# Activation sums of a down projection's seven-product pairs kept in device memory, with ten such pairs in each half in place of seven

## The chip, the core and the metric

The kernel runs on one core of a Trainium2 chip. The profile names the core's engines: PE (TensorE, matrix multiply, with its weight loads shown as PEld), DVE (VectorE, elementwise work), ACT (ScalarE, elementwise functions and copies), POOL (GpSimd; here masks and a DMA queue) and SP (SyncE; here only a DMA queue). Each engine takes its own instructions in order, and semaphores tie them together. Data moves between device memory and on-chip memory by DMA; products are accumulated in PSUM, on-chip memory of eight banks of 128 x 512 numbers as this kernel uses it.

The metric is device time in microseconds (us) of one execution, lower is better. A run of the kernel gives one time, and the time of a kernel is the median of its runs. One further execution is profiled, and all rows of the profile are from it.

## The reference

The kernel computes one layer of a hybrid encoder on 256 positions with 2048 features, in float32, and a last norm. The first part (gated mixing, neighbourhood attention, their merge) is not touched. What matters here is the second part:

```python
def conv_ffn(x, g_norm, w_up, conv_k, conv_b, w_down):
    h = rms_norm(x, g_norm)
    up = h @ w_up
    t = up.shape[1]
    pad = jnp.pad(up, ((0, 0), (1, 1), (0, 0)))
    up = (pad[:, :t] * conv_k[0] + pad[:, 1:t + 1] * conv_k[1]
          + pad[:, 2:t + 2] * conv_k[2] + conv_b)
    gate, val = jnp.split(up, 2, axis=-1)
    return x + (jax.nn.silu(gate) * val) @ w_down
```

`w_up` is 2048 x 11008, `w_down` 5504 x 2048. The down projection multiplies a 256 x 5504 matrix of activations by `w_down`.

## The kernel before

**Splitting.** Each float32 operand is split into a high part, rounded to the type that PE multiplies (`fp32r` in the profile), and a low part, the difference. A product is then three matmuls, high by high, low by high and high by low, all added in PSUM. That is `triple` (L289 to L293). For weights the split is made in `split_to` (L130): ACT copies the raw weights `wraw` into `whi`, DVE subtracts and writes `wlo` (L151 and L152). Four buffers of each (`SPLIT_AHEAD + 1`) hold split weights, five (`LOAD_AHEAD`) hold raw ones.

**Pieces.** All weights are loaded in one list of pieces, in the order in which they are used. A piece of the down projection is 128 rows of `w_down` by 1024 columns, kept as two blocks of 512 columns. `begin(i)` starts piece i: it issues loads up to piece i + 4 on SP's queue, the split of piece i + 3, and then the tasks that were set for i with `at(i, ...)`. After that PE's matmuls of piece i are recorded. This is what sets each engine's order: nothing is rescheduled.

**The down projection.** It is run by `wide` and `run_wide` in two halves of 1024 columns each (`g_dn`). A half has 43 pieces: 21 pairs and a single piece. Of the output, four blocks are accumulated: two blocks t of 128 positions by two blocks c of 512 columns, in four banks C. A plain piece is four triples, one for each block, 12 matmuls; a plain pair 24. A pair whose position is in `DOWN_QUADS` is computed with seven products instead of eight, in the manner of Strassen's method as Winograd arranged it: sums of the two pieces' weight blocks and sums of the two activation blocks are multiplied, and four more banks P collect four of the products over all such pairs of the half. Such a pair is 3 triples in its first piece and 4 in its second, 21 matmuls.

Before, seven pairs of each half are done so, at positions 4, 6, 9, 11, 14, 16, 18 and 3, 5, 8, 10, 13, 15, 17. For a pair that begins with piece i there is this work:

- `act_sums` at i - 5 on DVE: high and low of the activations are added again (L298), and four sums and differences of 128 x 128 blocks are made (L300 to L303);
- `act_sums_split` at i - 4: these are split, by ACT (L309) and DVE (L310);
- `weight_sums` at i - 3: four sums and differences of 512-column blocks, on DVE (L316 to L319);
- `weight_sums_split` at i - 2: two splits of 1024 columns, on ACT (L326) and DVE (L327);
- of the pair's own first piece only one of the two blocks is split (`units`).

All results go into eight rooms of `hpool` (`h_room`), one for each name, which held the input of the up projection before. After the last such pair, `ev_sums` takes the four products P from their banks and adds them into the output `x2` in two parts (L909 to L914, L917 to L919). At the end of the first half `ev_down` adds the four banks C, squares the result for the last norm and multiplies it by that norm's weights (`columns`, L1022), which are loaded through POOL's queue (`load_fin`, two buffers). The last four pieces of the second half are walked block by block (`tail`), so that each block can be finished while PE works on the next.

**The up projection** comes before it: 22 groups of eight pieces; `ev_up` takes a group's banks and makes the convolution, the gate (`gate`) and the split activations `ff["a"]` for two blocks of 128 features, as tasks of the next group's pieces.

Of the kernel before, what the change touches and what calls it, by code (L numbers as in the profile page):

```python
# [8 lines left out]
F32 = mybir.dt.float32  # L9
# [48 lines left out]
Y_GAP = 224  # L58
DOWN_QUADS = ((4, 6, 9, 11, 14, 16, 18), (3, 5, 8, 10, 13, 15, 17))


@with_exitstack
def trunk_kernel(ctx, tc, x, norm_mix, w_in, ln_g, ln_b, w_s, b_s, rpb, w_branch, w_out,
# [202 lines left out]

    def wide(src, row0, order, c0, acts, quads, room, done, sums=None, odd=None):
# [21 lines left out]
    def triple(p, x, h, l, st, sp):  # L289
# [3 lines left out]
        nc.tensor.matmul(p, xh, l, start=False, stop=sp)  # L293

    def act_sums(a, box, room):
        w = room("f", F32)
        f = w[:, 0].rearrange("p (k t) -> p k t", k=2)
        nc.vector.tensor_add(f, a[:, :, 0, :].bitcast(F32), a[:, :, 1, :].bitcast(F32))  # L298
        s1, s2, s3, s4 = (w[:, 1, n * 128:(n + 1) * 128] for n in range(4))
        nc.vector.tensor_add(s1, f[:, 0, 128:], f[:, 1, 128:])  # L300
        nc.vector.tensor_sub(s3, f[:, 0, :128], f[:, 0, 128:])
        nc.vector.tensor_sub(s2, s1, f[:, 0, :128])
        nc.vector.tensor_sub(s4, f[:, 1, :128], s2)  # L303
        box["w"] = w

    def act_sums_split(box, room, name):
        w = box.pop("w")
        o = room(name, F32R)
        nc.scalar.activation(o[:, 0], w[:, 1], AF.Copy)  # L309
        nc.vector.tensor_sub(o[:, 1], w[:, 1], o[:, 0].bitcast(F32))  # L310
        box["s"] = [(o[:, 0, n * 128:(n + 1) * 128], o[:, 1, n * 128:(n + 1) * 128]) for n in range(4)]

    def weight_sums(i, box, room):
        r0, r1 = whole.pop(i), whole.pop(i + 1)
        t13, t24 = room("t13", F32), room("t24", F32)
        nc.vector.tensor_sub(t13[:, 0], r0[:, 1], r0[:, 0])  # L316
        nc.vector.tensor_sub(t24[:, 0], r1[:, 1], t13[:, 0])
        nc.vector.tensor_sub(t13[:, 1], r1[:, 1], r0[:, 1])
        nc.vector.tensor_sub(t24[:, 1], r1[:, 0], t24[:, 0])  # L319
        box["w"] = (t13, t24)  # L320

    def weight_sums_split(box, room):
        u = []
        for name, t in zip(("13", "24"), box.pop("w")):
            h, l = room("h" + name, F32R), room("l" + name, F32R)
            nc.scalar.activation(h, t, AF.Copy)  # L326
            nc.vector.tensor_sub(l, t, h.bitcast(F32))  # L327
            u.append((h, l))
        box["t"] = {1: [x[:, 0] for x in u[0]], 3: [x[:, 1] for x in u[0]],
                    2: [x[:, 0] for x in u[1]], 4: [x[:, 1] for x in u[1]]}  # L330

    def run_wide(g, tail=0):
# [12 lines left out]
        for i in range(n0, n1 - tail):  # L345
# [22 lines left out]
            S, W = boxes[q]["acts"]["s"], boxes[q]["t"]  # L368
            triple(P[1], S[0], *W[1], st, sp)
            triple(P[3], S[2], *W[3], st, sp)  # L370
            triple(P[2], S[1], *W[2], st, sp)
            triple(C[1][0], x_of(k1, 1), *W[4], False, False)
# [152 lines left out]
    def post_sums(P, x, spare):  # L525
        p1, p5, p6, p7 = P
        (x11, x12), (x21, x22) = x
        nc.scalar.activation(x11, p1, AF.Copy)
        nc.vector.tensor_add(spare, p6, x11)
        nc.vector.tensor_add(x12, p5, spare)  # L530
        nc.vector.tensor_add(x21, p7, spare)
        nc.vector.tensor_add(x22, p5, x21)

    def add_sums(ps, x):
        for t in range(NT):
            for c in range(2):
                nc.vector.tensor_add(x[t][c], ps[t][c], x[t][c])

# [360 lines left out]
    def ev_sums(j, room):  # L899
        def done(P, i):  # L900
            x2 = rs["x2"]
            p1, p5, p6, p7 = P
            x11, x12, x21, x22 = (x2[:, t, c * 512:(c + 1) * 512] for t in range(2) for c in (j, j + 1))
            m = {}

            def first_half():
                ab, cd = room("t13", F32), room("t24", F32)
                m["v"], m["u3"], m["w"] = cd[:, 0], cd[:, 1], ab[:, 0]
                nc.scalar.activation(ab[:, 0], p1, AF.Copy)  # L909
                nc.vector.tensor_add(x11, p1, x11)  # L910
                nc.vector.tensor_add(ab[:, 1], p6, ab[:, 0])
                nc.vector.tensor_add(m["v"], p5, ab[:, 1])
                nc.vector.tensor_add(m["u3"], p7, ab[:, 1])
                nc.vector.tensor_add(m["w"], p5, m["u3"])  # L914

            def second_half():
                nc.vector.tensor_add(x12, x12, m["v"])  # L917
                nc.vector.tensor_add(x21, x21, m["u3"])
                nc.vector.tensor_add(x22, x22, m["w"])  # L919

            at(i + 1, first_half)
            at(i + 2, second_half)
        return done
# [49 lines left out]
    def ev_up(f0, nb):  # L973
        def done(ps, i):
            n = nb
            a = []
            for p in ps:
                t = tmp.tile([128, T], F32, name="tb", bufs=3)
# [45 lines left out]
    def ev_down(ps, i):  # L1024
# [111 lines left out]
    h_room = {n: f"h{i}" for i, n in enumerate(("t13", "t24", "h13", "h24", "l13", "l24", "f", "s"))}  # L1136
# [113 lines left out]
    ff["ap"] = [fa.tile([128, min(2, NF - k), 2, T], F32R, name=f"a{k // 2}") for k in range(0, NF, 2)]  # L1250
    ff["a"] = [ff["ap"][k // 2][:, k % 2] for k in range(NF)]
    fc = {}

# [4 lines left out]
    for g in g_up:  # L1258
        run_group(g)
    def open_fin():  # L1260
        fc["st"].close()
# [47 lines left out]
```

## Time and profile before

The kernel before took 1316.88 us, median of 3 runs (1316.34 to 1316.91). Of the profiled execution the page gives the span from the first to the last instruction.

| what | us |
|---|---|
| time, median of 3 runs | 1316.88 |
| span of the profiled execution | 1314.9 |
| PE busy | 1303.3 (99%) |
| DVE busy | 1066.2 (81%) |
| ACT busy | 764.8 (58%) |
| POOL busy | 88.3 (7%) |

Rows of a timeline or a group read: start in us or the line, how long, the engine, the line of the code, the operation, what is written and read by the program's names, the shape, and how many alike. Square brackets give how long the engine sat idle ahead of the row and what ended that. A row of the busy time by stretch has the stretch, its length, then for each engine the busy time and the number of instructions, the granted clock of PE (1.00 is full), the share of time in which the DMA engines were busy, and what they moved in GB/s. A line of the DMA table has the number of issues, the size of one and the median time to landing. A row's duration and the distance to the next row's start are two things, since instructions of one engine overlap a little.

### The profile page before, as it was taken

To read this page: it belongs to the slowest core of one execution; us is meant where nothing else is said; L and a number is where in the kernel's file an instruction comes from. 1 tells how busy PE (TensorE), PEld (TensorE's weight loads), DVE (VectorE), ACT (ScalarE), POOL (GpSimd) and SP (SyncE) were. 2 spreads that over 40 slices of the span, in tenths; PEclk is the share of its full clock that TensorE was granted. 3 is DMA by queue.
4 is the path that set the end of the run, shared out by engine and by line. 5 is a ranking of instruction groups with operands and counts; after the bars stand their busy time and mean duration, and the time that the engine had idled before them with its cause. 6 is when DMAs were issued, how large, how long until landed. Compare 5 with 4: busy or idle time off the path is not lost.

```text
span 1314.9 us, 19329 instructions
## 1 busy us (share of the span) xinstructions
PE 1303.3 (99%) x6776; PEld 1112.0 (85%) x6776; DVE 1066.2 (81%) x1625; ACT 764.8 (58%) x1139; POOL 88.3 (7%) x176
## 2 busy tenths in 40 slices
PE   9999999999999999999999999999999999999997
PEld 7888888888888888888888888888888888888885
DVE  7996778667789966986777778787878789999997
ACT  5766476666645644556555555555656556555653
POOL 0004505323000000000000000000000000000000
PEclk9999999999999999999999999999999999999999
DMA  8768656556556657665565665656565656666663
GB/s 305 260 209 235 201 174 201 181 163 194 179 172 209 210 190 241 204 210 163 175 202 182 192 193 182 195 184 193 180 205 177 198 154 226 220 194 206 210 202 119
DMA packets 170577, 259.37 MB, mean 197 GB/s; under 512 B 12664, under 2 KB 124144, under 8 KB 170480
## 3 DMA queue, kind: packets, MB, share of 16 engines
q1 hardware_dynamic: 166448, 250.31, 59.4%
q0 software_dynamic: 3712, 7.30, 2.4%
q8 instruction: 53, 0.87, 0.3%
q10 hardware_dynamic: 320, 0.53, 0.1%
q14 instruction: 44, 0.36, 0.1%
HBM read 253.90 MB, written 2.10 MB: 195 GB/s over the span
## 4 chain that ended last, share of the span: by engine, by line
PE 97%; DVE 1%; ACT 0%; issue 0%; DMA 0%; ACTq 0%; DVEq 0%
PE bank L205 31%; PE bank L209 16%; PE bank L293 12%; PE bank L291 12%; PE bank L292 12%; PE bank L233 5%; PE bank L235 4%; PE bank L234 4%; PE bank L761 1%; DVE wlo L152 0%; PE bank L811 0%; PE bank L503 0%; PE bank L627 0%; PE bank L801 0%; PE bank L892 0%
## 5 line engine op out<-in xcount | busy, mean ns | idle before, releaser
L152 DVE TENSOR_TENSOR wlo<-wraw,whi 128x1024 fp32r<-128x1024 f32 (+1 forms) x472 | 550.3, 1178 | 188.7 <-ACT whi L151 92.0
L151 ACT ACTIVATE whi<-wraw 128x1024 fp32r<-128x1024 f32 (+1 forms) x472 | 472.0, 1015 | 204.7 <-PE bank L292 75.2
L205 PE MATMUL bank<-h,whi 128*128 128x512 f32 x1760 | 426.0, 392 | 0.0
L205 PEld LDWEIGHTS bank<-h,whi 128*128 128x128 f32 x1760 | 321.9, 188 | 62.0 <-DVE ya L631 0.3
L209 PEld LDWEIGHTS bank<-h,wlo 128*128 128x128 f32 x1760 | 225.9, 191 | 8.8
L209 PE MATMUL bank<-h,wlo 128*128 128x256 f32 x1760 | 228.6, 283 | 0.0
L989 ACT ACTIVATE tc<-ta,ck 128x256 f32<-128x256 f32 x86 | 47.1, 594 | 117.1 <-DVE ta L987 117.1
L293 PE MATMUL bank<-wlo,a 128*128 128x512 f32 x260 | 101.5, 390 | 0.2 <-DVE wlo L152 0.2
L292 PE MATMUL bank<-whi,a 128*128 128x512 f32 x260 | 101.2, 389 | 0.0
L291 PE MATMUL bank<-whi,a 128*128 128x512 f32 x260 | 101.2, 389 | 0.0
L291 PE MATMUL bank<-whi,h 128*128 128x512 f32 x204 | 80.3, 393 | 0.0
L292 PE MATMUL bank<-whi,h 128*128 128x512 f32 x204 | 79.5, 390 | 0.0
L293 PE MATMUL bank<-wlo,h 128*128 128x512 f32 x204 | 79.5, 390 | 0.0
L293 PEld LDWEIGHTS bank<-wlo,a 128*128 128x128 f32 x260 | 48.8, 188 | 11.2 <-DVE wlo L152 1.3
L292 PEld LDWEIGHTS bank<-whi,a 128*128 128x128 f32 x260 | 48.8, 188 | 10.3
L291 PEld LDWEIGHTS bank<-whi,a 128*128 128x128 f32 x260 | 48.8, 188 | 10.1
L992 DVE SCALAR_TENSOR_TENSOR tc<-ta,ck,tc 128x255 f32<-128x255 f32 x86 | 41.4, 481 | 14.5 <-ACT tc L989 14.5
L979 ACT ACTIVATE tb<-bank 128x256 f32<-128x256 f32 x86 | 28.3, 385 | 42.2 <-PE bank L205 42.2
L233 PE MATMUL bank<-whi,y 128*128 128x512 f32 x128 | 50.5, 394 | 0.0
L233 PE MATMUL bank<-whi,h 128*128 128x512 f32 x128 | 50.4, 394 | 0.0
L235 PE MATMUL bank<-wlo,h 128*128 128x512 f32 x128 | 49.9, 390 | 0.0
L235 PE MATMUL bank<-wlo,y 128*128 128x512 f32 x128 | 49.9, 390 | 0.0
(299 smaller groups left out, 1744.1 us busy)
## 6 DMA issues: line engine op xcount, KB each, us to landing
wraw<-in_w_up_dram SPq DMA_DIRECT2D x336, 256.0 KB, 3.2
wraw<-in_w_in_dram SPq DMA_DIRECT2D x111, 512.0 KB, 4.5
wraw<-in_w_down_dram SPq DMA_DIRECT2D x86, 512.0 KB, 4.6
wraw<-in_w_in_dram SPq DMA_DIRECT2D x66, 256.0 KB, 3.2
wraw<-in_w_branch_dram SPq DMA_DIRECT2D x32, 512.0 KB, 4.5
wraw<-in_w_out_dram SPq DMA_DIRECT2D x32, 512.0 KB, 3.6
xs<-in_x_dram SPq DMA_DIRECT2D x8, 256.0 KB, 7.6
vw<-y POOLq DMA_DIRECT2D x16, 128.0 KB, 6.9
```

The costliest lines, as they stand in the source:

```text
L151: nc.scalar.activation(h[:, k, :m], w[:, k, :m], AF.Copy)
L152: nc.vector.tensor_sub(l[:, k, :m], w[:, k, :m], h[:, k, :m].bitcast(F32))
L205: nc.tensor.matmul(p, h[:, k - k0, b * 128:(b + 1) * 128], acts(k), start=k == 0, stop=k == nk - 1)
L209: nc.tensor.matmul(p[:, :T], l[:, k - k0, b * 128:(b + 1) * 128], acts(k)[:, 0, :], start=False, stop=False)
L233: nc.tensor.matmul(p, xh, h[:, kk, :m], start=st, stop=False)
L234: nc.tensor.matmul(p, xl, h[:, kk, :m], start=False, stop=False)
L235: nc.tensor.matmul(p, xh, l[:, kk, :m], start=False, stop=sp)
L291: nc.tensor.matmul(p, xh, h, start=st, stop=False)
L292: nc.tensor.matmul(p, xl, h, start=False, stop=False)
L293: nc.tensor.matmul(p, xh, l, start=False, stop=sp)
L989: nc.scalar.activation(v, u, AF.Identity, scale=ck[:, 1, ch:ch + 1], bias=ck[:, 3, ch:ch + 1])
L992: nc.vector.scalar_tensor_tensor(v[:, 1:], u[:, :T - 1], ck[:, 0, ch:ch + 1], v[:, 1:], op0=OP.mult, op1=OP.add)
```

## The change

Four things change, and they belong together.

1. The activation sums are made once, in the up projection. When the second block of a pair has been gated, `sums` (two pieces later) makes the four sums of 128 x 128 blocks from the gated activations before they are split, `sums_split` (one piece after that) splits them and stores them to device memory through POOL's queue, for the ten pairs of `DOWN_PAIRS`. The down projection no longer calls `act_sums`; `stored`, set for piece i - 4, loads 512 KB of split sums back, through POOL's queue, into one of two rooms in turn. Each stored pair is used in both halves.
2. Each half now has ten pairs with seven products, at positions 3, 5, 7, 9, 10, 12, 14, 16, 17, 19 and 2, 4, 6, 8, 9, 11, 13, 14, 16, 18. `down_order` arranges the pieces of a half so that the ten stored pairs come to these positions.
3. The split weight sums have two sets of rooms, used in turn (`both_rooms`); the second is a pool opened at the start of the down projection.
4. The signs of the sums are chosen anew (adds for subtractions among the weight sums, and the reverse where products are put together), with as many operations as before. The last norm's weights are loaded three pieces later, and the memory that is set aside for the descriptors of POOL's DMAs is set to 2048 bytes of each partition, where it was left at its default.

```diff
-DOWN_QUADS = ((4, 6, 9, 11, 14, 16, 18), (3, 5, 8, 10, 13, 15, 17))
+DOWN_PAIRS = (3, 5, 7, 9, 10, 12, 14, 16, 17, 19)
+DOWN_QUADS = (DOWN_PAIRS, (2, 4, 6, 8, 9, 11, 13, 14, 16, 18))
...
-            own = odd if odd and n % 2 else room
+            own = odd if odd and n % 2 else split_room or room
...
-            if sums is None:
+            if stored:
                 b["acts"] = {}
-                sum_acts_at(i - 5, i - 4, b["acts"], lambda k=order[2 * q]: ff["ap"][k // 2], room, "s")
+                at(i - 4, lambda b=b, k=order[2 * q]: stored(k // 2, b["acts"]))
...
+    def act_blocks(w, a11, a21, a12, a22):
+        s3, n1, p2, s4 = (w[:, n * 128:(n + 1) * 128] for n in range(4))
+        nc.vector.tensor_sub(s3, a11, a21)
+        nc.vector.tensor_sub(n1, a22, a21)
+        nc.vector.tensor_add(p2, n1, a11)
+        nc.vector.tensor_sub(s4, a12, p2)
...
     def weight_sums(i, box, room):
         r0, r1 = whole.pop(i), whole.pop(i + 1)
         t13, t24 = room("t13", F32), room("t24", F32)
-        nc.vector.tensor_sub(t13[:, 0], r0[:, 1], r0[:, 0])
-        nc.vector.tensor_sub(t24[:, 0], r1[:, 1], t13[:, 0])
-        nc.vector.tensor_sub(t13[:, 1], r1[:, 1], r0[:, 1])
-        nc.vector.tensor_sub(t24[:, 1], r1[:, 0], t24[:, 0])
+        nc.vector.tensor_add(t13[:, 0], r0[:, 0], r0[:, 1])
+        nc.vector.tensor_add(t24[:, 1], t13[:, 0], r1[:, 1])
+        nc.vector.tensor_add(t13[:, 1], r0[:, 1], r1[:, 1])
+        nc.vector.tensor_add(t24[:, 0], r1[:, 0], t24[:, 1])
...
+                own[b] = g
+                if b and f0 // 2 in ff["kept"]:
+                    at(cur[0] + 2, sums)
+                    at(cur[0] + 3, sums_split)
+
+            def sums():
+                own["w"] = ff["more"].tile([128, 512], F32, name="sw")
+                act_blocks(own["w"], *(own[k][:, t * 128:(t + 1) * 128] for k in range(2) for t in range(2)))
+
+            def sums_split():
+                o = ff["more"].tile([128, 2, 512], F32R, name="so")
+                split_plain(own["w"], o)
+                nc.gpsimd.dma_start(ff["kept"][f0 // 2], o.bitcast(F32))
...
-            fin["load"]()
+            at(cur[0] + 3, fin["load"])
...
+    def both_rooms(name, dt):
+        n = ff[name] = ff.get(name, -1) + 1
+        return (ff["twice"] if n % 2 else hpool).tile([128, 2, 512], dt, name=h_room[name])
+
+    def stored(pair, box):
+        n = ff["turn"] = ff.get("turn", -1) + 1
+        o = down_room(f"s{n % 2}", F32R)
+        nc.gpsimd.dma_start(o.bitcast(F32), ff["kept"][pair])
+        box["s"] = sums_of(o)
+
+    def down_order(g):
+        free = [p for p in range(NF // 2) if p not in DOWN_PAIRS]
+        kept = list(DOWN_PAIRS)
+        pairs = [(kept if q in DOWN_QUADS[g] else free).pop(0) for q in range(NF // 2)]
+        return tuple(2 * p + kk for p in pairs for kk in range(2)) + (NF - 1,)
+
-    g_dn = [wide(w_d, 0, range(NF), g * 1024, lambda k: ff["a"][k], DOWN_QUADS[g], down_room,
-                 (ev_sums(2 * g, down_room), ev_down if g == 0 else finish)) for g in range(2)]
+    g_dn = [wide(w_d, 0, down_order(g), g * 1024, lambda k: ff["a"][k], DOWN_QUADS[g], down_room,
+                 (ev_sums(2 * g, down_room), ev_down if g == 0 else finish), stored=stored, split_room=both_rooms) for g in range(2)]
+    dram = keep("dram", space=bass.MemoryType.DRAM)
+    ff["kept"] = {p: dram.tile([128, 2, 512], F32, name=f"sums{p}") for p in DOWN_PAIRS}
...
-    nc = _bacc.Bacc("TRN2", target_bir_lowering=False, num_devices=1)
+    nc = _bacc.Bacc("TRN2", target_bir_lowering=False, num_devices=1, dynamic_dma_scratch_size=2048)
```

More of the change, by code (lines that the diff above doesn't have):

```diff
@@ L262, in run_group, with wide @@
             done(ps, b)
-    def wide(src, row0, order, c0, acts, quads, room, done, sums=None, odd=None):
+    def wide(src, row0, order, c0, acts, quads, room, done, sums=None, odd=None, stored=None, split_room=None):
         n0 = plan_wide(src, row0, order, c0)
@@ L298, in act_sums @@
         nc.vector.tensor_add(f, a[:, :, 0, :].bitcast(F32), a[:, :, 1, :].bitcast(F32))
[L299 to L303, printed above, removed]
+        act_blocks(w[:, 1], *(f[:, k, t * 128:(t + 1) * 128] for k in range(2) for t in range(2)))
         box["w"] = w
@@ L310, in act_sums_split, with sums_of @@
         nc.vector.tensor_sub(o[:, 1], w[:, 1], o[:, 0].bitcast(F32))
-        box["s"] = [(o[:, 0, n * 128:(n + 1) * 128], o[:, 1, n * 128:(n + 1) * 128]) for n in range(4)]
+        box["s"] = sums_of(o)
+    def sums_of(o):
+        return [(o[:, 0, n * 128:(n + 1) * 128], o[:, 1, n * 128:(n + 1) * 128]) for n in range(4)]
     def weight_sums(i, box, room):
@@ L976, in done @@
             a = []
+            own = {}
             for p in ps:
@@ L1251, in trunk_kernel @@
     ff["a"] = [ff["ap"][k // 2][:, k % 2] for k in range(NF)]
+    ff["more"], more_st = pool("more")
     fc = {}
```

26 lines of the change are left out of this document (16 added, 10 removed).

## The prediction

> **What bounds the kernel now.** I read the chain of waits first, then the busy time by stretch, then the timelines of TensorE (PE) and VectorE (DVE) in the down projection.
>
> ```profile
> PE 97%; DVE 1%; ACT 0%; issue 0%; DMA 0%; ACTq 0%; DVEq 0%
> core 0: us, PE busy (x) PEld busy (x) DVE busy (x) ACT busy (x) POOL busy (x), PEclk, DMA share, GB/s
> 640.00:1080.00 440.00, 440.00 (x2533) 388.94 (x2532) 340.57 (x558) 249.24 (x399) 0.00 (x0) 1.00 0.60 186
> 1080.00:1195.00 115.00, 115.00 (x508) 94.94 (x508) 110.53 (x159) 64.76 (x78) 1.13 (x2) 1.00 0.67 219
> 1195.00:1315.00 120.00, 110.58 (x486) 90.67 (x484) 108.34 (x165) 63.82 (x84) 1.08 (x2) 0.98 0.54 178
> ```
>
> PE sets the end: 97% of the chain is matmuls. The last two stretches are the down projection. PE is never idle in the first of them, but DVE is busy 110.5 of 115 us, so a matmul taken away there is worth its time only if DVE keeps up. In the up projection (640 to 1080) DVE has 23% left.
>
> What a matmul costs is not its duration but the distance to the next one:
>
> ```profile
> 1281.11 0.39 PE L291 MATMUL bank<-whi,a 128*128 128x512 f32 x1
> 1283.15 0.39 PE L291 MATMUL bank<-h,h 128*128 128x512 f32 x1
> 1192.71 0.39 PE L291 MATMUL bank<-whi,a 128*128 128x512 f32 x1
> 1195.43 0.39 PE L291 MATMUL bank<-whi,a 128*128 128x512 f32 x1
> ```
>
> The first two rows are the first and the tenth matmul of a seven-product pair: 9 in 2.04 us, 0.227 each; rows of 0.39 overlap. The last two are the starts of two plain pieces, 12 matmuls in 2.72 us. So a plain pair of pieces takes PE 24 x 0.227 = 5.44 us, a seven-product pair 21 x 0.227 = 4.76.
>
> **What the change removes from PE.** 14 seven-product pairs become 20. Six pairs lose 3 matmuls each: 18 x 0.227 = 4.08 us off the engine that sets the end. This is the first term, if nothing comes in its place.
>
> **What it moves on DVE.** One seven-product pair, and what follows it, before:
>
> ```profile
> 1277.39 0.68 DVE L152 TENSOR_TENSOR wlo<-wraw,whi 128x512 fp32r<-128x512 f32 x1
> 1277.99 0.68 DVE L316 TENSOR_TENSOR h<-wraw 128x512 f32<-128x512 f32 x1
> 1280.52 1.22 DVE L152 TENSOR_TENSOR wlo<-wraw,whi 128x1024 fp32r<-128x1024 f32 x1
> 1281.66 2.35 DVE L327 TENSOR_TENSOR h<-h,h 128x1024 fp32r<-128x1024 f32 x2
> 1283.93 4.62 DVE L152 TENSOR_TENSOR wlo<-wraw,whi 128x1024 fp32r<-128x1024 f32 x4
> 1288.47 0.68 DVE L910 TENSOR_TENSOR x<-bank,x 128x512 f32<-128x512 f32 x1
> ```
>
> Again by starts: half split 0.60, four weight sums 2.53, second split 1.14, two splits of the sums 2.27, together 6.54 us from 1277.39 to 1283.93. A plain piece is one split, (1288.47 - 1283.93) / 4 = 1.135 us. The sums of activations stand beside that:
>
> ```profile
> 1167.23 0.69 DVE L298 TENSOR_TENSOR h<-a 128x512 f32<-128x512 f32 x1
> 1168.89 1.22 DVE L152 TENSOR_TENSOR wlo<-wraw,whi 128x1024 fp32r<-128x1024 f32 x1
> 1170.03 0.68 DVE L310 TENSOR_TENSOR h<-h,h 128x512 fp32r<-128x512 f32 x1
> 1170.63 0.68 DVE L152 TENSOR_TENSOR wlo<-wraw,whi 128x512 fp32r<-128x512 f32 x1
> ```
>
> 1.66 (L298 to L303) + 0.60 (L310) = 2.26 us for each pair. In the down projection DVE loses 14 x 2.26 = 31.6 us and gains 6 x (6.54 - 2 x 1.135) = 25.6: 6.0 us less, while PE takes 4.1 less. In total DVE is about as near to PE as before, so the order within the stage decides. Before, a seven-product pair and the plain pair after it cost DVE 6.54 + 2.26 + 2.27 = 11.07 us against 10.20 on PE; that lost 0.9 each time and was won back at a spacing of three. Now it is 8.81 against 10.20, a gain of 1.4. Only where two such pairs touch (positions 9 and 10, 16 and 17 of the first half, 8 and 9, 13 and 14 of the second) does DVE take 6.54 against 4.76 and fall back 1.8 us. DVE's order at the first touching place of the first half, as changed (wraw raw weights, whi and wlo their two parts, h the rooms of the sums):
>
> ```order
> L153 TENSOR_TENSOR wlo<-wraw,whi 128x512
> L323 TENSOR_TENSOR h_11483<-wraw 128x512
> L324 TENSOR_TENSOR h_11484<-h_11483,wraw 128x512
> L325 TENSOR_TENSOR h_11483<-wraw 128x512
> L326 TENSOR_TENSOR h_11484<-wraw,h_11484 128x512
> L153 TENSOR_TENSOR wlo<-wraw,whi 128x1024
> L334 TENSOR_TENSOR h_11508<-h_11483,h_11507 128x1024
> L334 TENSOR_TENSOR h_11512<-h_11484,h_11511 128x1024
> L153 TENSOR_TENSOR wlo<-wraw,whi 128x512
> L323 TENSOR_TENSOR h_11535<-wraw 128x512
> ```
>
> The second pair's half split now follows the first pair's last split at once; the second set of rooms lets it be written while PE still reads the first. Before, DVE had this between two pairs in the same half (a the activations):
>
> ```order
> L327 TENSOR_TENSOR h_11407<-h_11382,h_11406 128x1024
> L327 TENSOR_TENSOR h_11411<-h_11383,h_11410 128x1024
> L152 TENSOR_TENSOR wlo<-wraw,whi 128x1024
> L298 TENSOR_TENSOR h_11432<-a_5953 128x512
> L300 TENSOR_TENSOR h_11432<-h_11432 128x128
> L301 TENSOR_TENSOR h_11432<-h_11432 128x128
> L302 TENSOR_TENSOR h_11432<-h_11432 128x128
> L303 TENSOR_TENSOR h_11432<-h_11432 128x128
> L152 TENSOR_TENSOR wlo<-wraw,whi 128x1024
> L310 TENSOR_TENSOR h_11456<-h_11432,h_11456 128x512
> ```
>
> The two plain splits had the five steps of the activation sums and their split between them; all six are gone from here.
>
> How much DVE may fall back: it runs ahead of PE only as far as the four buffers of split weights let it.
>
> ```profile
> 1196.49 1.23 DVE L152 TENSOR_TENSOR wlo<-wraw,whi 128x1024 fp32r<-128x1024 f32 x1 [0.69 <-ACT whi L151]
> ```
>
> Here DVE had caught up: PE began piece 44 at 1195.43, ACT then split piece 47, and DVE began it 1.06 us after that start. From such a state I carry the sum through the first touching place, time 0 at PE's start of piece 15 (piece 18 begins position 9). PE starts 18 at 8.16, 20 at 12.92, 21 at 14.96. DVE: half split (after half that 1.06) and weight sums 0.6 to 3.75, next split and sums' split to 7.15, the second pair's to 10.3 and 13.7. The second pair's own split is done at 11.4 and needed at 14.05 (sixth matmul of piece 20); its sums are done at 13.7 and needed at 16.8. Some 2.6 us are left. The same sum for the start of the second half, where the four products with the final norm's weights (L1022) stand between the first two pairs, leaves 1.9. Before, the tightest place is in the rows already shown: the split that starts at 1280.52 ends at 1281.74, and the sixth matmul of the piece from 1281.11 starts at 1282.24, 0.50 us later. So the new order has more room than the old one, which did not stall, and I add nothing here. **Bounds**: 0 and 4 x (1.8 - 0.5) = 5.2 us, if DVE came to each touching place as late as at that tightest one. I take 0, since the rows that load it there are gone.
>
> **Start of the stage.** The first such pair moves from position 4 to 3.
>
> ```profile
> 1080.30 0.39 PE L291 MATMUL bank<-whi,a 128*128 128x512 f32 x1
> 1083.53 0.19 PEld L293 LDWEIGHTS bank<-wlo,a 128*128 128x128 f32 x1 [0.30 <-DVE wlo L152]
> 1092.53 1.22 DVE L152 TENSOR_TENSOR wlo<-wraw,whi 128x1024 fp32r<-128x1024 f32 x1
> 1095.33 0.42 DVE L486 TENSOR_TENSOR a<-tc,a 128x256 fp32r<-128x256 f32 x1
> ```
>
> The stall of 0.30 at piece 1 comes from the convolution's tail and stays. From 1092.53 DVE now does a half split (0.60), weight sums (2.53), the convolution's last step (L486, 0.42) and split 7 (1.14): done at 1097.2. PE needs it at the sixth matmul of piece 6, 1080.30 + 0.2 + 6 x 2.72 + 1.13 = 1098.0. It fits by 0.8; bounds 0 and 1.
>
> **End of the stage.** Four pieces are walked block by block there, 3 matmuls each, so the last splits are wanted quickly, and DVE is in the sums of the products (L910 to L919):
>
> ```profile
> 1291.72 1.22 DVE L152 TENSOR_TENSOR wlo<-wraw,whi 128x1024 fp32r<-128x1024 f32 x1
> 1292.85 0.69 DVE L917 TENSOR_TENSOR x<-x,h 128x512 f32<-128x512 f32 x1
> 1294.65 2.35 DVE L152 TENSOR_TENSOR wlo<-wraw,whi 128x1024 fp32r<-128x1024 f32 x2
> 1295.93 0.50 PE L293 MATMUL bank<-wlo,a 128*128 128x512 f32 x1
> 1297.07 0.50 PE L293 MATMUL bank<-wlo,a 128*128 128x512 f32 x1 [0.17 <-DVE wlo L152]
> 1305.36 0.39 PE L293 MATMUL bank<-wlo,a 128*128 128x512 f32 x1
> ```
>
> The two 0.50 rows should have started 0.227 after the matmuls ahead of them; they are 0.09 and 0.34 us late: 0.43 lost. DVE's order at the end before (h the rooms of the product sums, x the output):
>
> ```order
> L914 TENSOR_TENSOR h_12804<-bank,h_12805 128x512
> L152 TENSOR_TENSOR wlo<-wraw,whi 128x1024
> L917 TENSOR_TENSOR x_5242<-x_5242,h_12805 128x512
> L918 TENSOR_TENSOR x_5242<-x_5242,h_12805 128x512
> L919 TENSOR_TENSOR x_5242<-x_5242,h_12804 128x512
> L152 TENSOR_TENSOR wlo<-wraw,whi 128x1024 x2
> ```
>
> Two splits came behind the second half of the sums (L917 to L919), and PE waited for both. As changed:
>
> ```order
> L921 TENSOR_TENSOR h_12929<-bank,h_12930 128x512
> L153 TENSOR_TENSOR wlo<-wraw,whi 128x1024
> L924 TENSOR_TENSOR x_5254<-x_5254,h_12930 128x512
> L925 TENSOR_TENSOR x_5254<-x_5254,h_12930 128x512
> L926 TENSOR_TENSOR x_5254<-x_5254,h_12929 128x512
> ```
>
> No split is left behind it. Let T be PE's end of the last pair (position 18). Its first piece, ended at T - 2.72, releases the buffers of splits 40 and 41: two ACT steps of about 1 us and DVE's 1.14 end at T + 0.5. The first five sums (3.25 us, 1288.47 to 1291.72) run to T + 3.8, the last split to T + 4.9; PE wants it at T + 2.72 + 11 x 0.227 = T + 5.2. I take a stall of 0.1, a gain of 0.35; bounds 0.43 gained, 1.5 lost (if DVE comes 1.8 later, as it did before). The second half of the sums (1.8 us) then delays the first output block by about 1.1, which the second, 2.72 later, takes up.
>
> **The up projection** gets, for 10 of 22 groups, four 128x128 steps, a split of 512 (1.6 us of DVE, about 0.5 of ACT) and a 512 KB store.
>
> ```profile
> 819.74 1.23 DVE L152 TENSOR_TENSOR wlo<-wraw,whi 128x1024 fp32r<-128x1024 f32 x1
> 822.57 1.23 DVE L152 TENSOR_TENSOR wlo<-wraw,whi 128x1024 fp32r<-128x1024 f32 x1 [1.60 <-PE bank L209]
> ```
>
> These are the two pieces behind which the steps now stand. DVE sat idle 1.60 us between them, waiting for PE to free a buffer; the first 1.0 goes into that, the rest behind the second. Cost 0; without that cover 10 x 1.6 us at most, but the whole stretch has DVE at 340.6 of 440 us and PE never idle, so I keep that end out of the range.
>
> **The loads.** 20 sums of 512 KB come back through POOL's queue.
>
> ```profile
> L1272 POOL DMA_DIRECT2D gfin<-in_norm_final_dram x4: 537/548/572, 1092.9 to 1214.1; - x4
> DMA to landing us min/median/max: 3.6/5.2/6.1
> wraw<-in_w_down_dram SPq DMA_DIRECT2D x86, 512.0 KB, 4.6
> x<-in_x_dram POOLq DMA_DIRECT2D x4, 512.0 KB, 7.8
> DMA to landing us min/median/max: 6.4/7.8/10.4
> ```
>
> The nearest are the four loads of x, same size and queue but issued together, 6.4 to 10.4 us (last row), and those of the final norm's weights (second row). A sum's buffer is free after the ninth matmul of the second piece two such pairs back, and the sum is wanted at the seventh of the next one. At the tightest spacing (7 to 10) this is 0.7 + 5.44 + 4.76 + 1.4 = 12.3 us; less an issue of 0.7, 11.6. Cost 0. The final norm's later loads move three pieces on, so that none waits ahead of a sum.
>
> **Sum.** 1314.9 - 4.08 - 0.35 = 1310.5 us of span. The median lies 2.0 us over the span (1316.88), so 1312.5.
>
> **Rivals.**
> First, DVE falls behind at the touching places: for it, 96% busy; against it, the room worked out above. About half the bound, 2.6 us, comes back: 1315.1.
>
> Second, weights land late because the sums share the DMA engines. For it, a DMA share of 0.67, which 10.5 MB more in 220 us (48 GB/s on 219) lifts to about 0.8. Against it: the median landing of 4.6 us. A buffer is released by one split and used by the fifth after it; five pieces take at least 12 us, less 2.2 for the two steps of a split, some 10. If each sum pushed a weight by its own share (0.52 MB at 219 GB/s, 2.4 us), only the start and the four touching places could feel it, some 0.4 us each: 1314.5. The Trainium skill, "DMA: Bandwidth & Descriptors", section "Issuing engines are not separate DMA queues", says that DMAs issued from several engines run on the same 16 DMA engines and interleave; by that a second queue buys no bandwidth, and this rival is what it would cost.
>
> Third, the slower side: the sums come late. PE would stand in the first piece of a pair, at its third triple. The four tightest places have 11.6 us. From 12.7 us (1.1 late, four times) the gain is gone; at 14 us, 4 x 2.4 = 9.6 lost, 1322. For it, POOL shares the core with a DVE that never rests; against it, issues of 0.55 us and landings of 5.2 in just this stage. The Trainium skill, "SBUF — State Buffer", section "Who interferes with whom", warns that DVE can lock GpSimd out of a port that it needs to write descriptors, but names the two-port modes for that, which it says two-tensor operations do not have; the issues of 0.55 us agree.
>
> **Chances.** Forecast 0.68; first rival 0.13 (mostly no change); second 0.08 (half of it still faster); third 0.06; 0.05 for what I have not seen. A measurement here tells about 0.2%, 2.6 us, from no change. Faster 0.68 + 0.04 + 0.03 = 0.75, within it 0.16, slower 0.06 + 0.03 = 0.09. Range: 1311.5 (all of 0.43 and 0.30 regained, and 0.5 of scatter, as the three runs have) to 1316.3, which takes in the first two rivals and leaves out the third.
>
> **What would show it.** Right: 18 fewer rows of L292 to L294, PE still without idle time between 1085 and 1290, a down projection of about 221 us to the last matmul, no DMA among the releasers of PE, no stall above 0.2 before the last triples. Wrong: LDWEIGHTS rows waiting for DVE at positions 10, 17, 9 or 14 (first rival), ACT's splits waiting for DMA (second), PE waiting for a DMA at the third triple (third), or PE idle in the up projection.

## The result, and the profile after

The changed kernel takes 1311.92 us, the median of five runs (1311.67 to 1312.27), against 1316.88 (1316.32 to 1317.22) for the kernel before beside it: 0.9963 of the time, 95% interval 0.9951 to 0.9975. Its profiled execution took 1312.27 us with a span of 1310.5. The prediction said 1312.5, with a span of 1310.5, and 1311.5 to 1316.3.

The chain of waits by engine, and three rows of the DMA issues (KB each, median us from issue to landing), from the page of the changed kernel:

```profile
PE 98%; DVE 1%; ACT 0%; issue 0%; DMA 0%; ACTq 0%; DVEq 0%
...
wraw<-in_w_down_dram SPq DMA_DIRECT2D x86, 512.0 KB, 5.3
...
h<-sums POOLq DMA_DIRECT2D x20, 512.0 KB, 6.9
sums<-so POOLq DMA_DIRECT2D x10, 512.0 KB, 4.3
```

The busy time by stretch, with the columns of the prediction's first fence:

```profile
640.00:1080.00 440.00, 440.00 (x2534) 388.91 (x2533) 355.64 (x608) 255.60 (x408) 5.42 (x10) 1.00 0.63 198
1080.00:1195.00 115.00, 115.00 (x509) 95.01 (x508) 109.90 (x138) 67.61 (x78) 7.49 (x14) 1.00 0.82 278
1195.00:1310.00 115.00, 106.34 (x470) 87.67 (x468) 104.34 (x140) 64.25 (x82) 5.33 (x10) 0.98 0.65 220
```

PE still sets the end. In the up projection DVE has 15.1 us more (340.57 before) and PE loses nothing of its 440.00. In the first half of the down projection DVE is as full as it was (109.90 of 115, 110.53 before), and PE has no idle time. The DMA share is 0.82, where it was 0.67.

The waits in the down projection (us in total, times, longest), and the first and the last matmul of the stage from PE's timeline:

```profile
ACT whi L152 <- PE bank L293: 32.4, 20, 3.9
ACT whi L152 <- DMA wraw<-in_w_down_dram: 5.4, 7, 1.5
PEld bank L294 <- DVE wlo L153: 0.3, 1, 0.3
```
```profile
1080.63 0.39 PE L292 MATMUL bank<-whi,a 128*128 128x512 f32 x1
1300.95 0.39 PE L294 MATMUL bank<-wlo,a 128*128 128x512 f32 x1
```

The third row of the waits is all that PE's weight loads wait for in the whole stage: the stall of 0.30 at piece 1, which was there before. ACT now waits for a DMA seven times, for weights that come later; nothing of it reaches PE.

I call the time from the first to the last of these two matmuls the stage: 1300.95 - 1080.63 = 220.32 us, against 1305.36 - 1080.30 = 225.06 before. What follows the stage is the same 9.5 us in both profiled executions (1310.5 - 1300.95, 1314.9 - 1305.36). So the whole difference of the spans is 4.74 us less in the stage and 0.32 more ahead of it. The start of the stage lies between 1079.71 and 1080.63 in the profiled executions of all twelve kernels of this study, so the 0.32 is scatter; what a kernel does in the stage is read from the stage alone, which repeats far better than the whole time.

### The profile page after: what moved, and what is told of

It is laid out like the page before. It is cut to its first block, busy times and chain, and to the rows that moved or that the text cites. A ratio compares the mean times of both kernels' runs of the same rounds, so it can differ in the third digit from the quotient of the medians.

```text
span 1310.5 us, 19358 instructions
## 1 busy us (share of the span) xinstructions
PE 1299.2 (99%) x6758; PEld 1109.4 (85%) x6758; DVE 1076.5 (82%) x1627; ACT 774.2 (59%) x1147; POOL 104.5 (8%) x206
## 4 chain that ended last, share of the span: by engine, by line
PE 98%; DVE 1%; ACT 0%; issue 0%; DMA 0%; ACTq 0%; DVEq 0%
PE bank L206 31%; PE bank L210 16%; PE bank L292 12%; PE bank L293 12%; PE bank L294 12%; PE bank L234 5%; PE bank L236 4%; PE bank L235 4%; PE bank L768 1%; PE bank L818 0%; PE bank L510 0%; PE bank L634 0%; PE bank L808 0%; PE bank L899 0%; PE bank L971 0%
## 5 line engine op out<-in xcount | busy, mean ns | idle before, releaser
L294 PE MATMUL bank<-wlo,a 128*128 128x512 f32 x224 | 87.3, 390 | 0.0
L293 PE MATMUL bank<-whi,a 128*128 128x512 f32 x224 | 87.2, 389 | 0.0
L292 PE MATMUL bank<-whi,a 128*128 128x512 f32 x224 | 87.1, 389 | 0.0
L292 PE MATMUL bank<-whi,h 128*128 128x512 f32 x210 | 83.0, 395 | 0.0
L293 PE MATMUL bank<-whi,h 128*128 128x512 f32 x210 | 82.0, 391 | 0.0
L333 ACT ACTIVATE h<-h 128x1024 fp32r<-128x1024 f32 x40 | 40.2, 1053 | 33.8 <-DVE h L325 33.8
L234 PE MATMUL bank<-whi,y 128*128 128x512 f32 x128 | 50.5, 394 | 0.0
L234 PE MATMUL bank<-whi,h 128*128 128x512 f32 x128 | 50.4, 394 | 0.0
L235 PE MATMUL bank<-whi,y 128*128 128x512 f32 x128 | 49.8, 389 | 0.0
L235 PE MATMUL bank<-whi,h 128*128 128x512 f32 x128 | 49.8, 389 | 0.0
L294 PEld LDWEIGHTS bank<-wlo,a 128*128 128x128 f32 x224 | 42.0, 188 | 9.1 <-DVE wlo L153 0.3
```

What stands on the lines that cost most here:

```text
L234: nc.tensor.matmul(p, xh, h[:, kk, :m], start=st, stop=False)
L235: nc.tensor.matmul(p, xl, h[:, kk, :m], start=False, stop=False)
L292: nc.tensor.matmul(p, xh, h, start=st, stop=False)
L293: nc.tensor.matmul(p, xl, h, start=False, stop=False)
```

## The experiments

All times are medians, but two kernels ran once; stages are from the profiled executions. "Ratio" is against the kernel before on the same chip, with its 95% interval. Below, "margin" is the time from the end of a split on DVE to the start of the first matmul that reads it, and a "touching place" is where two seven-product pairs follow each other directly.

| Kernel | time, us | ratio | stage, us |
|---|---|---|---|
| before | 1316.88 | 1 | 225.06 |
| the change | 1311.92 | 0.9963 (0.9951 to 0.9975) | 220.32 |
| the change with the old positions | 1316.24 | 0.9996 (0.9988 to 1.0005) | 224.40 |
| the change with one set of rooms | 1311.91 | 0.9966 (0.9953 to 0.9978) | 220.33 |
| eleven pairs in each half | 1311.29 | 0.9957 (0.9945 to 0.9970) | 219.42 |
| twelve pairs in each half | 1319.80 | 1.0028 (1.0017 to 1.0038) | 227.99 |
| DVE's work of the sums put back | 1357.58 | one run | 266.19 |
| two loads of sums in place of 20 | 1312.29 | 0.9967 (0.9955 to 0.9980) | 220.32 |
| before, with the last pair at 18 | 1316.04 | 0.9994 (0.9985 to 1.0002) | 224.41 |
| one room for the loaded sums | 1340.94 | one run | 249.66 |
| eleven pairs, one set of rooms | 1313.22 | 0.9975 (0.9965 to 0.9985) | 221.34 |
| before, with the smaller descriptor memory | 1316.45 | 1.0000 (0.9991 to 1.0008) | 225.05 |

### The sums moved, the positions kept

```diff
-DOWN_PAIRS = (3, 5, 7, 9, 10, 12, 14, 16, 17, 19)
-DOWN_QUADS = (DOWN_PAIRS, (2, 4, 6, 8, 9, 11, 13, 14, 16, 18))
+DOWN_PAIRS = (4, 6, 9, 11, 14, 16, 18)
+DOWN_QUADS = (DOWN_PAIRS, (3, 5, 8, 10, 13, 15, 17))
```

> The change with the old positions: seven pairs in each half, the activation sums in device memory. The matmuls are those of before, DVE in the down projection has 14 x 2.26 = 31.6 us less. Theory (the gain is matmuls removed, DVE had kept up before): 1316.4 to 1316.9, as before, at most the 0.43 of the late triples at the end is gained; the stretch 1080 to 1195 shows DVE some 15 us less busy and PE as full as before. Rival (the gain is DVE's relief): 1314.9 or less. Rival (sums late or weights pushed, hidden behind the gain): 1317.4 or more.

The two stretches of the down projection, and the stage's first and last matmul:

```profile
1080.00:1195.00 115.00, 115.00 (x508) 95.00 (x508) 96.07 (x117) 62.37 (x71) 5.81 (x11) 1.00 0.78 262
1195.00:1310.00 115.00, 110.21 (x487) 90.91 (x485) 93.69 (x123) 60.78 (x77) 3.75 (x7) 0.99 0.60 199
```
```profile
1080.42 0.39 PE L292 MATMUL bank<-whi,a 128*128 128x512 f32 x1
1304.83 0.39 PE L294 MATMUL bank<-wlo,a 128*128 128x512 f32 x1
```

DVE is relieved by 14.5 us in the first stretch (110.53 before) and the time stays: 1316.24, just below what the theory expected. The stage is 0.65 us shorter than before. Against the change it is 224.40 - 220.32 = 4.08 us longer, which is 18 x 0.227 to the hundredth. So relief of DVE is worth those 0.65 us and no more by itself; what it does is to let six further pairs be had at no cost.

### DVE's work put back

```diff
+                at(i - 5, lambda k=order[2 * q]: same_work(ff["ap"][k // 2]))
+                at(i - 4, same_split)
...
```

The lines left out define the two: `same_work` makes the five sums on DVE, `same_split` copies on ACT and subtracts on DVE, all on one scratch tile.

> The change with DVE's and ACT's work of the activation sums put back into the down projection: for each of the 20 pairs five subtractions and additions and the split, written to a scratch tile that nothing reads (its result is unused). 20 x 2.26 = 45.2 us more on DVE in a stage of 220 us that has it busy 203 of them. Theory (ten pairs are possible only because the sums left DVE's path): DVE sets the end there, 25 to 36 us more, 1337 to 1348, weight loads waiting for DVE all along. Rival (DVE's busy time overstates its need, so that the store in device memory is needless): under 1320.

The waits of PE in the down projection:

```profile
PEld bank L305 <- DVE wlo L153: 37.0, 22, 3.5
PE bank L305 <- DVE wlo L153: 28.0, 19, 3.1
```

1357.58: the theory holds and its size was too low. DVE is now what PE waits for, 22 times in 20 pairs. The expectation had DVE busy 203 us of the change's stage; the profile has 209.55 of 220.32. In this kernel it is 256.16 of 266.19: 46.6 us more work, and a stage 45.9 longer. So DVE sets the whole length here, about 10 us of its idle time stay as they were, and every microsecond of sums put back costs one. PE's side of it: the spacings of successive matmuls beyond 0.227 add up to 36.3 us of waits, and to 8.9 us in 45 rows that stand 0.43 apart with no wait between them (the last section says what these are).

### Two loads of sums in place of twenty

```diff
-        o = down_room(f"s{n % 2}", F32R)
-        nc.gpsimd.dma_start(o.bitcast(F32), ff["kept"][pair])
+        if n < 2:
+            ff["s", n] = down_room(f"s{n % 2}", F32R)
+            nc.gpsimd.dma_start(ff["s", n].bitcast(F32), ff["kept"][pair])
+        o = ff["s", n % 2]
```

> 18 of the 20 loads of sums left out: the later pairs use the first two pairs' sums, so the output isn't the reference's. 9.4 MB less through the DMA engines in the down projection. Theory (the loads and what they push are hidden): 1311.4 to 1312.4, and the last matmul 220.3 us after the stage's first one, as in the change; ACT's 5.4 us of waits for the weights go away without moving the end. Rival (sums and weights sharing the DMA engines cost PE time): 1 us or more faster than the change.

From the page of this kernel:

```profile
wraw<-in_w_down_dram SPq DMA_DIRECT2D x86, 512.0 KB, 4.7
```

The weights land in 4.7 us again (4.6 before, 5.3 in the change) and ACT waits for none of them. The stage is that of the change to a hundredth of a us. So the loads do slow the weights, here by 0.6 us each in the median, and this costs PE nothing. The size is not firm: the other kernels with 20 or more loads have medians of 4.7 to 5.7.

### One room for the loaded sums

```diff
-        o = down_room(f"s{n % 2}", F32R)
+        o = down_room("s0", F32R)
```

> The change with one room for the loaded sums in place of two, so that a load starts when the pair just before has read its sums. From there to the need: 9 x 0.227 = 2.0 us where two pairs touch, 7.5 at a spacing of two. The loads landed in 5.2 to 8.7 us (median 6.9) in the change. Theory (the lead of 11.6 us that two rooms give is what hides the loads): 3.2 to 6.7 us lost at each of four touching places and 0 to 1.2 at the others, 1325 to 1345, about 1331, PE waiting for a DMA at the third triple of a pair. Rival (landings need less than the records say, so that the second room is needless): under 1316.

The waits of PE in the down projection:

```profile
PEld bank L292 <- DMA h<-sums: 21.4, 9, 5.3
PE bank L292 <- DMA h<-sums: 17.6, 7, 4.8
```

1340.94, 29.0 us more than the change, inside the range and above the middle of it. At the four touching places PE waited 3.2, 3.4, 4.8 and 3.5 us for the third triple (the row of the first stands in the last section), where the landing times gave 3.2 to 6.7; elsewhere the waits were 0 to 1.2. All spacings of successive matmuls beyond 0.227 make 21.1 us of waits, and 8.0 us come from 40 rows at 0.43 (the last section again). So the loads have a price, and the second room hides it: the lead counts, not the number of bytes.

### One set of rooms for the split weight sums

```diff
-                 (ev_sums(2 * g, down_room), ev_down if g == 0 else finish), stored=stored, split_room=both_rooms) for g in range(2)]
+                 (ev_sums(2 * g, down_room), ev_down if g == 0 else finish), stored=stored) for g in range(2)]
```

> The change with one set of rooms for the split weight sums. At the touching places the splits of the second pair's sums then wait for PE's last triples of the first pair. Theory (the second set pays only at the touching places): 0 to 1 us lost at each of four, so 1312 to 1315.2, with PE's weight loads waiting for DVE there and nowhere else; 1314.9 if the running balance that gives 0.74 at each is right. Rival (the old 2.6 us of room is large enough for one set as well): 1311.5 to 1312.3. Rival (the rooms are needed at every pair): 1317 or more.

1311.91, and a stage of 220.33: the rival was right, and with ten pairs the second set is worth nothing. The first touching place (positions 9 and 10), in the timelines of ACT, DVE and PE of this kernel:

```profile
1130.41 1.06 ACT L333 ACTIVATE h<-h 128x1024 fp32r<-128x1024 f32 x1 [2.33 <-PE bank L293]
...
1131.50 2.59 DVE L334 TENSOR_TENSOR h<-h,h 128x1024 fp32r<-128x1024 f32 x2 [1.56 <-ACT h L333]
...
1134.24 0.39 PE L294 MATMUL bank<-h,h 128*128 128x512 f32 x1
```

The split of the second pair's sums does wait for PE, 2.33 us on ACT and 1.56 on DVE. But the room of the first two sums is free six matmuls into the first pair's second piece (that piece starts at 1129.02, ACT at 1130.41), not at its end. The first split is done at 1132.72, 1.52 us before the first matmul that reads it. In the change the same split starts at once and is done 3.17 us ahead:

```profile
1129.49 1.22 DVE L153 TENSOR_TENSOR wlo<-wraw,whi 128x1024 fp32r<-128x1024 f32 x1
1130.63 2.35 DVE L334 TENSOR_TENSOR h<-h,h 128x1024 fp32r<-128x1024 f32 x2
```
```profile
1133.65 0.39 PE L294 MATMUL bank<-wlo,a 128*128 128x512 f32 x1
1135.01 0.39 PE L294 MATMUL bank<-h,h 128*128 128x512 f32 x1
```

DVE's own split at 1129.49 ends at 1130.71 and is needed at 1133.65, so the least margin at this place is 2.94 us. One set of rooms costs nothing because there is such margin: at the last touching place, where that of the change is 2.33 us, it leaves 1.05.

### Eleven pairs, with two sets and with one

```diff
+DOWN_PAIRS = (4, 5, 7, 9, 10, 12, 13, 15, 16, 18, 19)
+DOWN_QUADS = (DOWN_PAIRS, (2, 3, 5, 7, 8, 10, 12, 13, 15, 16, 18))
```

> Eleven pairs per half instead of ten (22 sums stored and loaded twice over, in other positions): 6 matmuls less, 6 x 0.227 = 1.36 us. DVE's load in the stage rises by 2 x (6.54 - 2.27) = 8.5 us. Theory (PE sets the end while DVE has some room at each touching place): 1310.5 to 1310.9. Rival (DVE's room is used up at ten): no gain, 1311.9 to 1313, with weight loads waiting for DVE at the touching places.

The one late row that is new, in PE's timeline:

```profile
1291.59 0.50 PE L294 MATMUL bank<-wlo,a 128*128 128x512 f32 x1 [0.18 <-DVE wlo L153]
```

1311.29 us, 0.6 less than the change, between the two expectations. No touching place stalls (the least margin is 0.4 us, at positions 7 and 8 of the second half), but DVE comes to the last four pieces 1.3 us later than in the change (4.3 us ahead of PE at the first of them, where it was 5.6). The last split, which was 0.21 us ahead in the change, is late, and 0.45 us are lost (0.34 by this row, 0.11 by the next). The stage says the same: 220.32 - 6 x 0.227 + 0.45 = 219.41, measured 219.42. The intervals of the two ratios overlap; it is by its stage, not by its median, that this version is the fastest of the study.

The same with one set of rooms (the edit shown above for ten pairs):

> Eleven pairs per half with one set of rooms for the split weight sums. With one set, ten pairs left 1.5 us between the second pair's split sums and PE's need of them, at the first three touching places alike: there PE's reading of the first pair sets the split's time, not DVE's lead. With eleven pairs DVE comes within 0.6 to 2.5 us of PE at the touching places with two sets. Theory (the one set costs DVE at most what is above 1.5 at each touching place, and a spacing of two wins 1.4 back): the time of eleven pairs with two sets, 1311.29, to 0.6 us more. Rival (losses add up from place to place once both limits are near): 1 to 4 us more, weight loads waiting for DVE in the second half.

The waits of PE in the down projection:

```profile
PEld bank L294 <- DVE wlo L153: 3.2, 6, 0.9
PE bank L294 <- DVE wlo L153: 0.6, 2, 0.4
```

1313.22, and 1.92 us more of stage than with two sets: the rival is right. Besides the stall at piece 1 there are five stalls, one at the end of the first half, three in the second half and one at the last pieces. One set costs nothing while DVE arrives early, and costs at once where the margin is already used.

### Twelve pairs

```diff
+DOWN_PAIRS = (3, 4, 6, 7, 9, 10, 12, 13, 15, 16, 18, 19)
+DOWN_QUADS = (DOWN_PAIRS, (2, 3, 5, 6, 8, 9, 11, 12, 14, 15, 17, 18))
```

> Twelve pairs per half, two then one piece pair apart in turn: 12 matmuls less than the change, 2.7 us by PE alone (1309.2). DVE: 24 pairs need 24 x 6.54 + 38 x 1.135 = 200 us and the evacuations, the norm's and the convolution's work some 30 us more, against 217 on PE. Theory (DVE becomes the bound): PE waits for DVE through the stage and the time is that of the change or worse, 1312 to 1320, about 1317 by the running balance. Rival (PE is the bound still): 1309 to 1310.

The waits of PE's weight loads and matmuls in the down projection, and two of PE's late rows:

```profile
PEld bank L294 <- DVE wlo L153: 12.3, 15, 2.5
PE bank L294 <- DVE wlo L153: 5.3, 6, 2.0
```
```profile
1118.67 0.50 PE L294 MATMUL bank<-wlo,a 128*128 128x512 f32 x1
...
1134.03 0.50 PE L294 MATMUL bank<-wlo,a 128*128 128x512 f32 x1
```

1319.80, slower than before: DVE is the bound. One touching and one spaced pair cost DVE 2 x 6.54 + 2.27 = 15.35 us by the prediction's rows and PE 2 x 4.76 + 5.44 = 14.96. From 1118.67 to 1180.09 five late rows follow one another at 15.35 or 15.36 us, DVE's time for the two pairs, and each costs 0.36 us (0.25 late, and 0.11 in the row behind), close to the 0.39 by which the two engines differ. Single stalls of 1.1, 1.65 and 2.2 us stand at the start, in the second half behind the evacuation of the first, and at the end.

### The end of the stage

```diff
-DOWN_QUADS = ((4, 6, 9, 11, 14, 16, 18), (3, 5, 8, 10, 13, 15, 17))
+DOWN_QUADS = ((4, 6, 9, 11, 14, 16, 18), (3, 5, 8, 10, 13, 15, 18))
```

> The kernel before with the second half's last seven-product pair at position 18 in place of 17, all else as before. Theory of the prediction (the late triples at the end come from two splits standing behind the product sums, and 18 leaves none there): some 0.4 us less of the stage, 1316.3, no PE row waiting for DVE after 1290. Rival (the late triples come from a DVE that has no lead left at the end, as the unmoved positions with a lighter DVE already lost them): 0.2 us less to 1.5 more, DVE waited for by PE near the end.

DVE at the end of this kernel, and then of the change:

```profile
1293.88 0.69 DVE L914 TENSOR_TENSOR h<-bank,h 128x512 f32<-128x512 f32 x1
1295.25 1.23 DVE L152 TENSOR_TENSOR wlo<-wraw,whi 128x1024 fp32r<-128x1024 f32 x1 [0.68 <-ACT whi L151]
1296.39 0.68 DVE L917 TENSOR_TENSOR x<-x,h 128x512 f32<-128x512 f32 x1
```
```profile
1289.96 0.69 DVE L921 TENSOR_TENSOR h<-bank,h 128x512 f32<-128x512 f32 x1
1291.34 1.23 DVE L153 TENSOR_TENSOR wlo<-wraw,whi 128x1024 fp32r<-128x1024 f32 x1 [0.69 <-ACT whi L152]
1292.49 0.68 DVE L924 TENSOR_TENSOR x<-x,h 128x512 f32<-128x512 f32 x1
```

In both, DVE has caught up before the last split (it waits 0.7 us for ACT) and no split stands behind the second half of the sums; no matmul is late after 1290. The stage is 0.65 us shorter, and 0.63 of that arises at the four rows from 1295.93 to 1297.40 of before. The median, 0.7 us less with an interval that holds 1, can't show so little. With the old position 17 and a lighter DVE the same 0.65 was won (first experiment). So the order that the prediction named cures the stall, and so does a DVE with lead: each alone is enough.

### The smaller descriptor memory

```diff
-    nc = _bacc.Bacc("TRN2", target_bir_lowering=False, num_devices=1)
+    nc = _bacc.Bacc("TRN2", target_bir_lowering=False, num_devices=1, dynamic_dma_scratch_size=2048)
```

> The kernel before with the smaller memory for POOL's DMA descriptors that the change sets, nothing else. Theory (few loads go through POOL's queue and none is on PE's path): no change, 1316.4 to 1317.0. Rival (POOL's loads of x and y at the start wait for room): 0.3 us or more slower, arising in the first 100 us, as the change's down projection began 0.32 us later than that of before.

No change: 1316.45 beside 1316.39 in the same series, and its stage begins at 1079.91, earlier than before's.

## Why the prediction was right, step by step

- **18 matmuls x 0.227 = 4.08 us.** Right to the hundredth, by the stages of the change and of the kernel with the old positions. The stage has 972 matmuls in place of 990.
- **Nothing added at the touching places.** Right. The margin was put at 2.6 us for the first one and is 2.94 there (2.3 at the places of the second half); at the start of the second half it was put at 1.9 and is 1.3. DVE's work in the stage was to fall by 6.0 us and fell by 4.95 (214.50 to 209.55). The reason given with it was only half right: the rows of the activation sums had to go, as the 45 us of the second experiment show, but the second set of rooms, which the prediction named as what lets the second pair's split be written, isn't needed at ten pairs.
- **Start of the stage.** The stall of 0.30 at piece 1 stayed, and the earlier pair fits: 0.75 us of margin, 0.8 predicted.
- **End of the stage.** The mechanism was right, and the size too small: a gain of 0.35 was predicted, 0.65 came. The 0.43 counted how late two rows start, 1295.93 and 1297.07. The next rows of the kernel before, in PE's timeline:

```profile
1296.27 0.40 PE L291 MATMUL bank<-whi,a 128*128 128x512 f32 x1
...
1297.40 0.39 PE L291 MATMUL bank<-whi,a 128*128 128x512 f32 x1
```

Each comes 0.33 to 0.34 us after the late one in place of 0.227, which makes another 0.2. And the stall of 0.1 taken for the new order did not come: the last split ends at 1292.57, 0.21 us before PE reads it.

- **Up projection.** Right: DVE has 15.1 us more (10 x 1.5) inside its idle time.
- **Loads of sums.** Cost 0, right; the price without the lead is the 29.0 us of the one-room kernel.
- **Sum.** 4.08 + 0.65 = 4.73 us less in the stage, 0.30 more than the sum said. That the span came out at 1310.5 all the same is chance: the stage of this execution began 0.32 us late. The other four runs have spans of 1309.9 to 1310.4.

Of the rivals, the first (DVE falls behind) is what happens at eleven pairs with one set and at twelve with two, not at ten. The second had its cause right and its effect not: the weights do land later, ACT does wait for them, 5.4 us in all, and the buffers between ACT and PE cover it. The Trainium skill's rule that was set beside it ("DMA: Bandwidth & Descriptors", section "Issuing engines are not separate DMA queues") agrees with the landings of 4.6 us without the loads on another engine's queue, 5.3 with them and 4.7 with two of the 20. The third, sums that come late, came about at a lead of 2.0 us in place of 11.6. Its descriptors were never held up: POOL's 20 issues took 531 to 540 ns each beside a DVE that is busy 95% of the stage.

## What to carry to other kernels

Cost a removed matmul at the distance between two of them, and ask of the engine behind it not how busy it is but how early it arrives at each place: here 95% busy with margins of 0.2 us and more behind the first pieces cost nothing, and two pairs more per half cost 7.7 us. Work that depends on neither half of a stage can be done where its engine idles and kept in device memory, if the way back has a lead above its landing time; a second room for the load gave that lead, a second set of rooms for the split weight sums did not matter until the margin was gone. Measure small terms in the stage that they change: from first to last matmul it repeated to 0.02 us between kernels with the same work, while whole times scatter by 0.6 or more.

## What the hardware showed that was not expected

A long wait of PE can cost more than its length. In the kernel with one room for the loaded sums, PE's rows after a wait at a touching place, and the stretches around them (the third number from the end is the granted clock):

```profile
1138.94 0.79 PE L292 MATMUL bank<-whi,h 128*128 128x512 f32 x1 [3.17 <-DMA h<-sums]
1139.53 0.63 PE L293 MATMUL bank<-whi,h 128*128 128x512 f32 x1
1139.96 0.63 PE L294 MATMUL bank<-wlo,h 128*128 128x512 f32 x1
```
```profile
1139.00:1145.20 6.20, 6.20 (x15) 4.85 (x16) 4.00 (x4) 2.95 (x3) 0.48 (x1) 0.51 0.77 265
1145.20:1150.00 4.80, 4.80 (x23) 3.93 (x22) 0.80 (x1) 1.06 (x1) 0.05 (x1) 1.00 0.36 126
```

After 3.17 us of waiting the granted clock is 0.51 for 6.2 us: matmuls take 0.63 us and stand 0.43 apart, 15 of them in 6.2 us in place of 3.4, 2.8 us more. Then the clock is whole again. No further wait follows for 30 us that could make up for it, so this loss stays. In the kernel with DVE's work put back, PE's rows after two waits of 2.73 us, and after the wait that came next behind each:

```profile
1135.42 0.50 PE L305 MATMUL bank<-wlo,a 128*128 128x512 f32 x1 [2.73 <-DVE wlo L153]
...
1142.57 0.50 PE L305 MATMUL bank<-wlo,a 128*128 128x512 f32 x1 [0.48 <-DVE wlo L153]
...
1178.44 0.50 PE L305 MATMUL bank<-wlo,a 128*128 128x512 f32 x1 [2.73 <-DVE wlo L153]
...
1185.58 0.50 PE L305 MATMUL bank<-wlo,a 128*128 128x512 f32 x1 [2.05 <-DVE wlo L153]
```

Slow rows follow the first wait, 0.7 us after it, and none the second. Yet the next late row comes 7.15 us behind the one and 7.14 behind the other: the wait there is 0.48 us after the slow rows and 2.05 without them. So where DVE sets the pace, slow rows of PE only shorten its next wait. Of the two kernels whose stages came out 8 to 9 us over their waits, only the one with one room for the loaded sums lost that time to the clock.

Which waits halve the clock? In these two kernels the clock is at half for 3.41 us at a time (or twice that), and in each kernel these times begin whole multiples of 3.41 us apart. Here are stretches cut at such times, in the kernel with DVE's work put back (the second number is PE's busy time):

```profile
1132.45:1135.86 3.41, 0.68 (x4) 0.39 (x3) 3.27 (x7) 2.90 (x5) 0.00 (x0) 1.00 0.43 154
1135.87:1139.28 3.41, 3.41 (x10) 2.64 (x9) 3.41 (x5) 0.50 (x1) 0.00 (x0) 0.50 0.51 154
...
1173.41:1176.82 3.41, 2.30 (x11) 1.57 (x9) 3.27 (x7) 2.00 (x2) 0.00 (x0) 1.00 0.57 204
1176.82:1180.24 3.42, 1.80 (x8) 1.48 (x9) 3.39 (x5) 2.10 (x3) 0.00 (x0) 1.00 0.42 113
...
1183.65:1187.06 3.41, 1.48 (x6) 1.24 (x7) 3.41 (x5) 3.24 (x4) 0.00 (x0) 1.00 0.77 243
1187.07:1190.48 3.41, 3.41 (x9) 2.63 (x8) 3.31 (x6) 0.65 (x1) 0.00 (x0) 0.50 0.67 215
```

The first wait of 2.73 us falls into one stretch, and the clock is halved in the next; the second is shared by two stretches, 1.11 us idle in one and 1.61 in the other, and the clock stays whole. In the three kernels with waits above 1.2 us (these two and twelve pairs) each of the ten stretches of the down projection with 1.93 us or more of PE idle is followed by one at half clock, and of the stretches at full clock none with 1.91 or less is. That this is a fixed limit is not shown. The Trainium skill ("TensorE: Matmul & The Clock Gate", section "What's actually happening") has PE's clock at half after an idle window of about 3.4 us, in windows that run on their own. The half clock and the stretches of 3.41 us agree with these rows; that such a window has to be idle throughout does not, since 1.93 us of idle time in one were enough.
